# Three spacer tiles in SBUF that move the start addresses of a matmul kernel's tiles

## The chip, the cores and the metric

The kernel runs on one core of a Trainium2 chip. The metric is the device time of one execution in microseconds (us), lower is better.

## The reference

Two transformer-like parts run one after the other on 256 tokens of width 1024, in float32.

```python
h = h + hybrid_mixer(rmsnorm(h, norm1_w), w_in, ...)   # part 1: dilated attention and a state-space scan side by side
h = h + swiglu(rmsnorm(h, norm2_w), w_ffn_in, w_ffn_out)
...
# part 2: two layers over a stream x and a context c (256 tokens each), each layer:
# modulated rms_norm -> swiglu -> joint attention (kinds a, b, c, d) -> modulated rms_norm -> swiglu
def swiglu_2(h, w_gate, w_up, w_down):
    return (jax.nn.silu(h @ w_gate) * (h @ w_up)) @ w_down
```

Nearly all of the arithmetic is in the products `activations @ weights`: the input and output projections of the mixers and the three matrices of each swiglu, about 360 MB of weights, each read once.

## The kernel before

Activations lie feature by feature: a tile of 128 features holds a stream's 256 tokens as 256 columns of 4 bytes, 1024 bytes in each partition. Where the streams x and c go through the same weights, their columns lie side by side and a matmul has 512 columns (2048 bytes); a single stream makes 256.

A float32 product is made as three float32r matmuls. Weights and activations are each split into a high and a low part, `h` (ScalarE copies, L114 and L119) and `lo` (VectorE subtracts, L115 and L120), and `mm3_k` adds three products into one PSUM tile:

```python
nc.tensor.matmul(out, h[:, c], ah, start=first, stop=False)    # L133
nc.tensor.matmul(out, h[:, c], al, start=False, stop=False)    # L134
nc.tensor.matmul(out, lo[:, c], ah, start=False, stop=last)    # L135
```

The first tile is stationary (128 weight columns of 4 bytes, 512 bytes a partition), the second is moving. A unit of the program is one 512 KB slab of weights: a DMA from SyncE's queue into `wraw`, the split into `wh` and `wl`, and 8 steps of three matmuls. `run` writes the units in order and prepares two or three ahead. Five buffers each of `wraw`, `wh` and `wl` allow this. Between units it weaves attention, norms and, from the end of part 1 on, background work (the modulation vectors, L981).

Moving tiles are named after what they hold: `ah`/`al` are the normed activations, `hh`/`hl` a swiglu's hidden values, `aoh`/`aol` the attention's output in part 1, `ynh`/`ynl` three of the four groups of the scan's normed output in part 1 (the fourth reuses `aoh`/`aol`), `hq`/`lq` and `hk`/`lk` low-rank queries and keys in part 2. The products of the value projections (L1145 to L1147) are the other way round: activations are stationary and a weight slice of 256 or 320 columns moves. Attention itself uses plain float32 matmuls, with `q`, `k`, `pts`, `e`, `xdt` and the like.

SBUF is given out by pools. Each pool is a stretch of bytes in every partition, the next one begins where the last ended (rounded up to 32 bytes), and tiles follow each other within it. So the size of one small tile sets where all the tiles of later pools begin. Order of the pools: `cst`, `raw`, `wsplit`, `tmp`, `small`, then the streams, then those of a block that is under way (`block1` opens `b1a` with `ah`/`al` and `b1x`, which begins with `cw`).

Of the kernel before, what the change touches and what calls it, by code (L numbers as in the profile page):

```python
# [8 lines left out]
F32 = mybir.dt.float32  # L9
# [39 lines left out]
class Unit:  # L49


    def __init__(self, src, at, n, body, streams=None, lin=None, wide=False):
        self.src, self.at, self.n, self.body, self.streams, self.lin = src, at, n, body, streams, lin
        self.wide = wide
# [14 lines left out]
class Builder:  # L69
    def __init__(self, ctx, tc, A):  # L70
        self.tc, self.nc, self.A, self.ctx = tc, tc.nc, A, ctx
        nc = self.nc
        self.cst = self.pool(ctx, "cst", 1)
        self.raw_p = self.pool(ctx, "raw", 5)
        self.w_p = self.pool(ctx, "wsplit", 5)
        self.tp = self.pool(ctx, "tmp", 10)
        self.small = self.pool(ctx, "small", 2)
        self.comb, self.one_p = None, None
        self.ps = ctx.enter_context(tc.tile_pool(name="ps", bufs=4, space=PSUM))
        self.pa = ctx.enter_context(tc.tile_pool(name="pa", bufs=2, space=PSUM))  # L80
        self.pt = ctx.enter_context(tc.tile_pool(name="pt", bufs=2, space=PSUM))
        self.dram = ctx.enter_context(tc.tile_pool(name="scratch", bufs=1, space=DRAM))
        self.X, self.ACT, self.acc, self.bg, self.deferred = {}, {}, {}, [], []

        self.ones = self.cst.tile([128, 128], F32, name="ones")
        nc.vector.memset(self.ones, 1.0)
        self.cols = self.cst.tile([128, NCOL], F32, name="cols")
        self.ident = self.cst.tile([128, 128], F32, name="ident")

    def pool(self, ctx, name, bufs):  # L90
        return ctx.enter_context(self.tc.tile_pool(name=name, bufs=bufs))
# [357 lines left out]
def block1(K, start_mod):  # L449
    nc, tc, A = K.nc, K.tc, K.A  # L450
    ctx = ExitStack()
    K.one_p = K.pool(ctx, "b1a", 1)
    xpool = K.pool(ctx, "b1x", 1)
# [22 lines left out]

    tri = K.cst.tile([128, 128], F32, name="tri")
    nc.gpsimd.dma_start(tri, A["tri"])
    cw = xpool.tile([128, 120], F32, name="cw")
    at, _ = COLS["conv_w"]  # L480

    y_t = [xpool.tile([128, 4, T], F32, name=f"y{g}") for g in range(4)]
# [1191 lines left out]
def kernel(ctx, tc, A, parts=(1, 2)):  # L1674
# [20 lines left out]
    if 1 in parts:  # L1695
        block1(K, start_mod)
    else:
        start_mod()
# [198 lines left out]
```

## Time and profile before

| | before |
|---|---|
| median of 3 runs | 2523.09 us (2517.67 to 2523.85) |
| the profiled execution: its time | 2521.26 us |
| its span in the trace | 2519.5 us |
| TensorE (PE) matmul busy | 2459.8 us, 98% |
| weight loads (PEld) busy | 2122.6 us, 84% |
| VectorE (DVE) busy | 1642.6 us, 65% |
| ScalarE (ACT) busy | 1069.2 us, 42% |
| granted TensorE clock, mean | 0.986 |

A matmul's own duration covers its way through the array and overlaps with the next one's, and its end is modelled. What a matmul costs in a dense stream is therefore read as the distance from its start to the next one's start, and that is called its step below. Over a longer stretch it is the first and last start divided by the number of steps between.

### The profile page before, as it was taken

What the parts mean: (1) busy time and instruction counts of PE and PEld (TensorE: products, weight loads), DVE (VectorE), ACT (ScalarE), POOL (GpSimd) and SP (SyncE); (2) the same over time, 40 slices, a digit from 0 to 9 for tenths busy, and PEclk for the clock granted to TensorE, in tenths of its full rate; (3) what the DMA queues carried; (4) which work ended last, traced back from release to release, by engine and by line L of the source; (5) the groups of instructions that cost most, each with busy time, mean ns of one, the idle gap of its engine ahead of it and who ended that gap; (6) DMA issues with size and microseconds to landing.
All of it is one profiled execution on the core that took longest, in us unless ns stands there. A gap on an engine that the chain in (4) does not pass through costs nothing.

```text
span 2519.5 us, 38382 instructions
## 1 busy us (share of the span) xinstructions
PE 2459.8 (98%) x15104; PEld 2122.6 (84%) x15104; DVE 1642.6 (65%) x3009; ACT 1069.2 (42%) x1934; POOL 20.6 (1%) x30
## 2 busy tenths in 40 slices
PE   6999999999999999999999999999999999999999
PEld 6999999999988888886598888887888888866999
DVE  4667877787855665768667666657545455767554
ACT  4557565535522222436743222243222234555443
POOL 1000000000000000000000000000000000000000
PEclk9999999999999999999899999999999999999999
DMA  8545555676444554331024555434555422332553
GB/s 249 151 153 162 160 163 185 209 251 205 160 154 142 167 175 127 120 118 51 1 61 158 166 159 159 155 95 145 176 166 159 146 88 74 108 89 80 176 185 126
DMA packets 117252, 363.83 MB, mean 144 GB/s; under 512 B 21170, under 2 KB 28658, under 8 KB 117072
## 3 DMA queue, kind: packets, MB, share of 16 engines
q1 hardware_dynamic: 114512, 355.73, 44.4%
q0 software_dynamic: 1280, 3.45, 0.7%
q8 instruction: 119, 1.95, 0.3%
q10 hardware_dynamic: 1280, 2.20, 0.3%
q14 instruction: 61, 0.50, 0.1%
HBM read 359.33 MB, written 3.82 MB: 144 GB/s over the span
## 4 chain that ended last, share of the span: by engine, by line
PE 71%; DVE 2%; ACT 1%; issue 0%; DMA 0%; ACTq 0%
PE pm L133 21%; PE pm L134 21%; PE pm L135 20%; PE pt L1120 1%; PE pm L1319 1%; PE pa L1027 1%; PE pt L1051 1%; PE pa L1571 1%; PE pa L1335 1%; PE pm L1579 1%; PE pm L1259 0%; PE pa L1296 0%; PE pm L1601 0%; PE pm L1145 0%; PE pa L1147 0%; PE pa L1145 0%
## 5 line engine op out<-in xcount | busy, mean ns | idle before, releaser
L133 PE MATMUL pm<-ah,wh 128*128 128x256 f32 (+2 forms) x3096 | 1012.5, 329 | 21.6 <-ACT ah L355 11.2
L134 PE MATMUL pm<-al,wh 128*128 128x256 f32 (+2 forms) x3096 | 1007.8, 326 | 1.2 <-DVE al L356 1.2
L135 PE MATMUL pm<-ah,wl 128*128 128x256 f32 (+2 forms) x3096 | 1005.2, 325 | 0.0
L114 ACT CAST wh<-wraw 128x1024 fp32r<-128x1024 f32 (+4 forms) x535 | 540.5, 1013 | 1045.7 <-PE pm L134 853.9
L115 DVE TENSOR_TENSOR wl<-wraw,wh 128x1024 fp32r<-128x1024 f32 (+4 forms) x535 | 627.4, 1176 | 253.2 <-ACT wh L114 250.9
L133 PEld LDWEIGHTS pm<-ah,wh 128*128 128x128 f32 (+1 forms) x3096 | 587.9, 191 | 81.6 <-ACT ah L355 12.9
L134 PEld LDWEIGHTS pm<-al,wh 128*128 128x128 f32 (+1 forms) x3096 | 590.5, 191 | 54.4 <-DVE al L356 2.4
L135 PEld LDWEIGHTS pm<-ah,wl 128*128 128x128 f32 (+1 forms) x3096 | 590.4, 191 | 51.6 <-issue 1.4
L134 PE MATMUL pm<-hl,wh 128*128 128x512 f32 (+1 forms) x934 | 317.5, 340 | 0.0
L133 PE MATMUL pm<-hh,wh 128*128 128x512 f32 (+1 forms) x934 | 316.8, 339 | 0.0
L135 PE MATMUL pm<-hh,wl 128*128 128x512 f32 (+1 forms) x934 | 316.5, 339 | 0.0
L981 DVE SCALAR_TENSOR_TENSOR junk<-wraw,cactc 128x1024 f32<-128x1024 f32 x112 | 137.1, 1224 | 182.1 <-DMA wraw<-w_mod 181.9
L981 DVE SCALAR_TENSOR_TENSOR junk<-wraw,cactx 128x1024 f32<-128x1024 f32 x144 | 176.0, 1222 | 42.9 <-DMA wraw<-w_mod 40.3
L135 PEld LDWEIGHTS pm<-hh,wl 128*128 128x128 f32 x934 | 176.0, 188 | 21.1
L134 PEld LDWEIGHTS pm<-hl,wh 128*128 128x128 f32 x934 | 175.9, 188 | 21.2
L133 PEld LDWEIGHTS pm<-hh,wh 128*128 128x128 f32 x934 | 175.7, 188 | 21.2
L119 ACT CAST hh<-g 128x512 fp32r<-128x512 f32 (+1 forms) x113 | 59.2, 526 | 175.0 <-DVE g L413 174.9
L413 DVE TENSOR_TENSOR g<-g,pm 128x512 f32<-128x512 f32 (+1 forms) x113 | 64.0, 566 | 69.6 <-PE pm L135 68.1
L120 DVE TENSOR_TENSOR hl<-g,hh 128x512 fp32r<-128x512 f32 (+1 forms) x113 | 63.9, 567 | 0.3
L443 DVE SCALAR_TENSOR_TENSOR xc<-pm,mcol0c,xc 128x256 f32<-128x256 f32 x56 | 27.0, 481 | 56.0 <-PE pm L135 55.8
L409 ACT ACTIVATE g<-pm 128x512 f32<-128x512 f32 (+1 forms) x116 | 56.0, 488 | 2.5 <-PE pm L135 2.3
L1120 PEld LDWEIGHTS pt<-ident,e 128*128 128x128 f32 x272 | 30.7, 144 | 21.8 <-issue 18.7
(422 smaller groups left out, 2249.3 us busy)
## 6 DMA issues: line engine op xcount, KB each, us to landing
wraw<-w_mod SPq DMA_DIRECT2D x144, 512.0 KB, 3.9
wraw<-f1g SPq DMA_DIRECT2D x44, 512.0 KB, 4.0
wraw<-f1u SPq DMA_DIRECT2D x44, 512.0 KB, 4.1
wraw<-f2g SPq DMA_DIRECT2D x44, 512.0 KB, 3.6
wraw<-f2u SPq DMA_DIRECT2D x44, 512.0 KB, 3.8
wraw<-f1d SPq DMA_DIRECT2D x32, 512.0 KB, 3.9
wraw<-f2d SPq DMA_DIRECT2D x32, 512.0 KB, 3.6
wraw<-w_xbc SPq DMA_DIRECT2D x24, 512.0 KB, 3.6
```

Of the source, the lines that this page charges most:

```text
L114: nc.scalar.copy(h[:, :f], raw[:, :f])
L115: nc.vector.tensor_tensor(lo[:, :f], raw[:, :f], h[:, :f].bitcast(F32), op=ALU.subtract)
L119: self.nc.scalar.copy(h, src)
L120: self.nc.vector.tensor_tensor(lo, src, h.bitcast(F32), op=ALU.subtract)
L133: nc.tensor.matmul(out, h[:, c], ah, start=first, stop=False)
L134: nc.tensor.matmul(out, h[:, c], al, start=False, stop=False)
L135: nc.tensor.matmul(out, lo[:, c], ah, start=False, stop=last)
L409: nc.scalar.activation(half(g["g"], s), p, AF.Silu)
L413: nc.vector.tensor_tensor(t, t, p, op=ALU.mult)
L443: self.nc.vector.scalar_tensor_tensor(x, p, gate, x, op0=ALU.mult, op1=ALU.add)
L981: nc.vector.scalar_tensor_tensor(junk, raw, 1.0, K.cact[s], op0=ALU.mult, op1=ALU.mult, accum_out=K.mcol[layer, s][:, j:j + 1])
L1120: nc.tensor.transpose(p[:, j * 128:(j + 1) * 128], b, K.ident)
```

## The change

Three tiles that nothing reads are put in: 320 bytes in a pool of their own behind the weight buffers, and 160 and 352 bytes behind `cw` in `block1`, where `cw` itself grows from 480 to 512 bytes (160 + 352 = 512). VectorE fills each once, so that it counts as written.

```diff
         self.w_p = self.pool(ctx, "wsplit", 5)
+
+        self.gap(self.pool(ctx, "gap", 1), 320)
         self.tp = self.pool(ctx, "tmp", 10)
...
+    def gap(self, pool, n):
+
+        self.nc.vector.memset(pool.tile([128, n // 4], F32, name=f"gap{n}"), 0.0)
...
-    cw = xpool.tile([128, 120], F32, name="cw")
+    cw = xpool.tile([128, 128], F32, name="cw")[:, :120]
+    K.gap(xpool, 160)
+    K.gap(xpool, 352)
     at, _ = COLS["conv_w"]
```

Where the tiles begin in the built program, as the remainder of the address by 512 bytes (and by 1024 for those that the text needs); a tile's 256-column blocks follow at 1024 or 2048 bytes, so they begin at the same remainder:

| tiles | before | after |
|---|---|---|
| `wraw`, `wh`, `wl` (weights; stationary in L133 to L135, moving in L1145 to L1147) | 0xc0 | 0xc0 |
| `ah`, `al`, `hh`, `hl`: moving | 0x40 (by 1024: 0x40) | 0x180 (by 1024: 0x180) |
| `aoh`, `aol`: moving | 0x20 (by 1024: 0x220) | 0x180 |
| `ynh`, `ynl`: moving | 0x180 (by 1024: 0x380) | 0xe0 |
| `hq`, `lq`, `hk`, `lk`: moving | 0x60 | 0x1a0 |
| moving slices of `wh`, `wl`, 320 columns (by 1024) | 0xc0, 0x1c0, 0x2c0 | the same |
| part 1's `q`, `k`, `vt`, `pts`, `xdt`, `la` (float32) | 0x180 | 0xe0 |
| part 2's `e`, `pts` (float32) | 0xc0 or 0x120 | 0x0 or 0x60 |

The order of the instructions on the engines stays as it was, except on VectorE at the very start of the program. There the rows of the kernel before are (`ones` and `rel` are constants, `acc` and `sq` the first norm's sums):

```order
L86 MEMSET ones 128x128
L466 MEMSET rel 33x24
L879 MEMSET half 128x1
L946 MEMSET one 128x1
L889 TENSOR_SCALAR cw<-cols 128x120
L307 TENSOR_TENSOR acc<-acc,sq 128x256 x4
```

In the changed kernel the same place reads (line numbers behind the new lines are 2 to 8 higher):

```order
L94 MEMSET gap_67 128x80
L88 MEMSET ones 128x128
L472 MEMSET rel 33x24
L94 MEMSET gap_134 128x40
L94 MEMSET gap_136 128x88
L887 MEMSET half 128x1
L954 MEMSET one 128x1
L897 TENSOR_SCALAR cw<-cols 128x120
L313 TENSOR_TENSOR acc<-acc,sq 128x256 x4
```

Three fills are added ahead of the first work that waits for data; no other instruction is added, removed or moved.

## Rows read from the trace of the kernel before

**Rows 1.** The page: busy time by engine, and the chain that ended last.

```profile
span 2519.5 us, 38382 instructions
...
PE 2459.8 (98%) x15104; PEld 2122.6 (84%) x15104; DVE 1642.6 (65%) x3009; ACT 1069.2 (42%) x1934; POOL 20.6 (1%) x30
...
PE 71%; DVE 2%; ACT 1%; issue 0%; DMA 0%; ACTq 0%
PE pm L133 21%; PE pm L134 21%; PE pm L135 20%; PE pt L1120 1%; PE pm L1319 1%; PE pa L1027 1%; PE pt L1051 1%; PE pa L1571 1%; PE pa L1335 1%; PE pm L1579 1%; PE pm L1259 0%; PE pa L1296 0%; PE pm L1601 0%; PE pm L1145 0%; PE pa L1147 0%; PE pa L1145 0%
```

**Rows 2.** Waits: who waited, for whom; us in total, times, longest us.

```profile
ACT wh L114 <- PE pm L134: 853.9, 311, 7.1
...
PE pm L133 <- ACT ah L355: 11.2, 9, 1.6
```

**Rows 3.** Matmul groups of L133 by shape: count, busy us, mean ns, idle before.

```profile
L133 PE MATMUL pm<-ah,wh 128*128 128x256 f32 x1968 | 567.1, 292 | 21.6 <-ACT ah L355 11.2 <-ACT q L526 8.3 <-ACT ah L119 2.0
...
L133 PE MATMUL pm<-hh,wh 128*128 128x256 f32 x460 | 129.8, 282 | 0.0
...
L133 PE MATMUL pm<-aoh,wh 128*128 128x256 f32 x64 | 18.6, 291 | 0.3 <-ACT aoh L119 0.3
...
L133 PE MATMUL pm<-ynh,wh 128*128 128x256 f32 x96 | 26.7, 279 | 0.0
...
L133 PE MATMUL pm<-ah,wh 128*128 128x512 f32 x1112 | 440.5, 396 | 0.0
...
L133 PE MATMUL pm<-hh,wh 128*128 128x512 f32 x474 | 187.1, 395 | 0.0
```

**Rows 4.** Timeline of TensorE, 256 columns moving from 0x40: first and 25th start.

```profile
560.14 0.28 PE L133 MATMUL pm<-ah,wh 128*128 128x256 f32 x1
...
563.02 0.28 PE L133 MATMUL pm<-ah,wh 128*128 128x256 f32 x1
```

**Rows 5.** Windows: us; busy us (instructions) of PE, PEld, DVE, ACT, POOL; clock; DMA share, GB/s.

```profile
300.00:400.00 100.00, 99.00 (x878) 94.86 (x877) 82.06 (x160) 63.52 (x120) 0.00 (x0) 1.00 0.49 155
500.00:600.00 100.00, 100.00 (x836) 100.00 (x835) 83.58 (x128) 43.60 (x61) 0.00 (x0) 1.00 0.75 252
700.00:1000.00 300.00, 300.00 (x1292) 243.24 (x1291) 185.26 (x281) 75.63 (x93) 0.00 (x0) 1.00 0.48 152
...
2400.00:2500.00 100.00, 100.00 (x846) 100.00 (x844) 56.48 (x71) 43.31 (x62) 0.00 (x0) 1.00 0.54 173
```

**Rows 6.** Timeline, one unit: 0x180 (first, 26th), then 0x20 (first, 12th).

```profile
399.00 0.28 PE L134 MATMUL pm<-ynl,wh 128*128 128x256 f32 x1
...
401.83 0.28 PE L135 MATMUL pm<-ynh,wl 128*128 128x256 f32 x1
401.95 0.28 PE L133 MATMUL pm<-aoh,wh 128*128 128x256 f32 x1
...
403.25 0.28 PE L135 MATMUL pm<-aoh,wl 128*128 128x256 f32 x1
```

**Rows 7.** Timeline, 320 columns of weights moving: first and 23rd start.

```profile
1126.74 0.31 PE L1145 MATMUL pm<-wh,ah 128*128 128x320 f32 x1
...
1129.96 0.31 PE L1146 MATMUL pm<-wh,al 128*128 128x320 f32 x1
```

**Rows 8.** Timeline, 512 columns from 0x40: first and 25th start.

```profile
803.67 0.39 PE L133 MATMUL pm<-ah,wh 128*128 128x512 f32 x1
...
809.25 0.40 PE L133 MATMUL pm<-ah,wh 128*128 128x512 f32 x1
```

**Rows 9.** A window at the lower clock, columns as in rows 5.

```profile
2156.90:2158.60 1.70, 1.70 (x9) 1.70 (x9) 0.94 (x2) 0.00 (x0) 0.00 (x0) 0.50 0.54 165
```

**Rows 10.** Timeline of that window, 256 columns from 0x60: first and 8th start.

```profile
2156.91 0.41 PE L134 MATMUL pm<-lq,wh 128*96 128x256 f32 x1
...
2158.40 0.41 PE L135 MATMUL pm<-hq,wl 128*96 128x256 f32 x1
```

**Rows 11.** A fill on VectorE: duration ns min/median/max, first and last start us.

```profile
L86 DVE MEMSET ones<- x1: 165/165/165, 0.8 to 0.8; 128x128 f32 x1
```

## The prediction

> **What bounds the kernel now.** I read the page first. TensorE is busy for 98% of the span, the three lines of the split product hold 62% of the chain that ended last, and no other engine has more than 2% of it [rows 1]. The waits say the same from the other side: the longest wait for TensorE is ScalarE's, 853.9 us in which the next weights' split could start and the weight buffer is still in use by a matmul, while TensorE's longest own wait sums to 11.2 us [rows 2]. So the time is, to a few per cent, the number of matmuls times the step from one start to the next, and I looked for what sets that step.
>
> The groups give the counts [rows 3]. Each of L133, L134 and L135 has as many. With 256 columns and a start that the change moves to 0x180 there are (1968 + 460 + 64) x 3 = 7476 matmuls, with 512 columns (1112 + 474) x 3 = 4758.
>
> The steps come from the timeline. 256 columns from 0x40: 2.88 us over 24 steps, 120.0 ns [rows 4]; later, 846 matmuls are seen in 100 us, two of them cut by the window's ends, so about 118.5 ns [rows 5]. I use 119.2. [...]
>
> The telling rows are in one unit at 399 us. Weights, engines and the second operand's place are the same, only the moving tile changes: `ynh` and `ynl`, which begin at 0x180, step by 2.83 us / 25 = 113.2 ns, and `aoh` and `aol` right behind them, at 0x20, by 1.30 / 11 = 118.2 ns [rows 6]. Weight slices of 320 columns, from 0xc0 and its neighbours, take 3.22 us / 22 = 146.4 ns where the columns are 133.3: 13.1 ns too many [rows 7]. So 0x20, 0x40 and 0xc0 cost 11.5 to 13 ns over the columns, 0x180 costs 6.6. That the start is the cause is an inference from four starts. 512 columns were only seen from 0x40 in bulk: 5.58 us / 24 = 232.5 ns, 19.2 over the 213.3 of the columns [rows 8].
>
> [...]
>
> **The change, part by part.**
>
> *256 columns from 0x180.* The row is there: 113.3 ns for 119.2. That is 5.9 x 7476 = 44.1 us.
>
> *512 columns from 0x180.* No row shows it. The least gain that fits the mechanism: the gain of 5.9 comes once a matmul, so 226.6 ns, which is also twice 113.3; that is 28.1 us. The most: the columns alone, 213.3 ns, 19.2 x 4758 = 91.4 us. Which of the two is nearer? From 0x40 the excess grows from 12.5 ns at 256 columns to 19.2 at 512, so part of it goes with the columns, about 6.7 per 256, and the rest, near 6, comes once. From 0x180 256 columns have 6.6 in all, which leaves room for one of these two parts and not for both. Between the matmuls a new stationary tile has to be taken in whatever the start, so I take it that the once-a-matmul part stays and the part that goes with the columns vanishes: 213.3 + 6.7 = 220.0 ns, 12.5 x 4758 = 59.5 us.
>
> *`ynh` and `ynl` leave 0x180* for 0xe0, where nothing was measured. If 0xe0 is like the other starts they lose what the rest gain: 96 x 3 x 5.9 = 1.7 us. At the other end they lose nothing.
>
> *Plain float32 matmuls* (attention, head sums) get other starts too, some leaving 0x180. They are lines of 1% of the chain or less, about 125 us together [rows 1]; a twentieth of that either way is 6 us. I take 0, since no row separates their starts.
>
> *Weights and the value projections* stay at 0xc0: 0.
>
> *Three fills on VectorE.* The largest fill now takes 165 ns [rows 11], so three smaller ones are under 0.5 us. They run while the first loads are on their way, hence 0; uncovered they cost 0.5.
>
> *What is given back.* A faster TensorE asks sooner for weights. In the dense stretches of 512 columns VectorE has 185.3 of 300 us and DMA a share of 0.48, so nothing is near its limit. Around 300 to 600 us VectorE is at 82 to 84%, and at 500 to 600 us DMA at 0.75 with 252 GB/s [rows 5]. From 100 to 640 us there are about 8.4 matmuls a us, 4500, which gain 27 us. If VectorE set the pace there all 27 would be lost, if the buffers bridge its bursts none. It would go from 84 to 88%, so I take a quarter, 7 us.
>
> Sum: 44.1 + 59.5 - 1.7 - 7 = 94.9 us. Against the profiled execution, 2521.3 us, this gives 2426.4; the median of the runs shown is 1.8 above it, so 2428 us.
>
> [...]
>
> **The rivals.**
>
> 1. *The forecast*: both widths gain, 512 by more than 256. About 2428 us.
> 2. *512 gains just 5.9 ns*, since the loss is at the start of a matmul and the growth with columns stays. For it: twice 113.3 is 226.6. Against it: the excess at 0x180 would then have no fixed part at all. 59.5 becomes 28.1: 2459 us.
> 3. *512 gains nothing*: its loss is another one than that of 256, as its different excess allows. 2428 + 59.5 = 2487 us.
> 4. *Nothing happens*: the step of `ynh` comes from something else, its place high in the partition or its four-block tiles. For it: there is one quick tile pair only. Against it: `hq`, as high and at 0x60, is not quick, though the stretch quoted for it is at the lower clock. 2523 us. [...]
> 5. *Slower*: the pattern repeats over 1024 bytes, not 512. The quick tiles stood at 0x380 by 1024, the new ones will stand at 0x180, half a turn away, and could be as far above today's step as 0x380 is below it: 5.9 x (7476 + 4758) = 72 us more, 2595. It decides as soon as the step from 0x180 lies over 119.2 and 232.5 ns. Against it: the 320-column slices begin at three places by 1024, and their 22 steps in a row average the same excess as the rest [rows 7], so no place of 1024 stood out among the slow ones.
>
> **How the numbers follow.** Rival 1 has 58%, 2 has 21%, 3 has 7%, 4 has 8%, 5 has 6%. The predicted time is the first's. Its own range comes from the 512 step at 216 (19 us less) to 224 ns (19 more) and from 0 to 20 us given back: 2402 to 2460. The range of 8 in 10 is carried up to take in rival 2 with half of those 27 us given back, 2459 + 7 = 2466, and a little for the float32 lines: 2402 to 2470; it leaves out rivals 3, 4 and 5, 21%. A measurement here tells about 0.3%, 7.6 us, from no change. Rivals 1, 2 and 3 are faster by more than that: 0.86. Rival 4 is no change: 0.08. Rival 5 is slower: 0.06.
>
> **What would show it.** In the profile after, steps of 113 ns in the 256-column stretches at 500 to 600 us (some 880 matmuls per 100 us, for 836) and in the last 100 us; 220 ns in the 512-column ones (some 1360 in 300 us for 1292, where 226.6 would give 1325); `ynh` slower than now, near 119, and `aoh` quicker. If ScalarE's wait for TensorE shrinks and TensorE's waits for `wh` or `wl` grow between 100 and 640 us, the given-back term is right in kind. The forecast is wrong if the 512 step stays over 228, or if VectorE's or DMA's lateness at 300 to 600 us eats the first term.

## The result, and the profile after

The changed kernel takes 2509.48 us (median of 11 runs, 2498.57 to 2517.63) where the kernel before takes 2522.72 us (11 runs, 2516.40 to 2529.99). The ratio is 0.9946, with a 95% interval of 0.9931 to 0.9962: 13 us faster. Forecast were 2428 us, 95 us faster, with a range that ends at 2470. The direction was right, the size was not. The profiled execution of the changed kernel took 2511.2 us and has a span of 2509.1, 10.4 us less than before [rows 1]. The same lines stand 6 higher now: L139, L140 and L141 are the matmuls that were L133 to L135.

The page of the changed kernel reads as it did before. TensorE is still the bound.

```profile
span 2509.1 us, 38385 instructions
...
PE 2440.5 (97%) x15104; PEld 2097.5 (84%) x15104; DVE 1641.9 (65%) x3012; ACT 1067.5 (43%) x1934; POOL 20.6 (1%) x30
...
PE 69%; DVE 4%; ACT 2%; issue 1%; DMA 0%; ACTq 0%; DVEq 0%; SPq 0%
PE pm L139 20%; PE pm L140 20%; PE pm L141 20%; PE pt L1128 1%; PE pa L1035 1%; DVE wl L121 1%; PE pm L1327 1%; PE pt L1059 1%; PE pa L1579 1%; PE pm L1587 1%; DVE al L362 1%; PE pa L1343 1%; DVE y L357 1%; PE pm L1267 1%; PE pa L1304 0%
```

The windows of the changed kernel (columns as in rows 5) show by stage what became of the two large terms.

```profile
500.00:600.00 100.00, 96.79 (x830) 95.66 (x829) 84.23 (x129) 43.53 (x62) 0.00 (x0) 1.00 0.75 253
700.00:1000.00 300.00, 300.00 (x1287) 241.71 (x1286) 182.83 (x276) 75.93 (x93) 0.00 (x0) 1.00 0.48 152
2400.00:2500.00 100.00, 100.00 (x851) 100.00 (x851) 56.69 (x74) 42.11 (x59) 0.00 (x0) 1.00 0.52 159
```

With 512 columns (700 to 1000 us) there are 1287 matmuls in 300 us where there were 1292 [rows 5]: the step grew. At the end, 851 for 846: the 256-column step shrank by 0.7 ns only. From 500 to 600 us there are 830 for 836, fewer than before, and TensorE is no longer busy all the time.

The timeline of TensorE in the changed kernel gives the steps: two stretches of 256 columns and one of 512, each by its first start and the start 18 steps on.

```profile
610.35 0.28 PE L139 MATMUL pm<-ah,wh 128*128 128x256 f32 x1
...
612.39 0.28 PE L139 MATMUL pm<-ah,wh 128*128 128x256 f32 x1
...
801.44 0.39 PE L139 MATMUL pm<-ah,wh 128*128 128x512 f32 x1
...
805.64 0.39 PE L139 MATMUL pm<-ah,wh 128*128 128x512 f32 x1
...
2400.42 0.28 PE L140 MATMUL pm<-al,wh 128*128 128x256 f32 x1
...
2402.54 0.28 PE L140 MATMUL pm<-al,wh 128*128 128x256 f32 x1
```

The same tile at the same start steps by 2.04 / 18 = 113.3 ns near 610 us and by 2.12 / 18 = 117.8 ns near 2400 us. 256 columns have two states, and only one is the row of `ynh` on which the forecast rested [rows 6]. 512 columns step by 4.20 / 18 = 233.3 ns, which is no gain at all over [rows 8].

Over the whole trace I took each step that is at most a quarter longer than its columns, at the 26.7 ns for 64 columns that *The step by columns* measures, and called what is longer a stall; its excess is what it has over its columns. The moved 256-column matmuls went from a mean of 119.0 to 115.7 ns, which over 7476 of them is -25 us. The 512-column ones went from 232.7 to 233.3: +3 us. `ynh` and `ynl` went from 113.9 to 116.8: +0.8. The stalls' excess went from 80.8 to 90.5: +9.7. These make -11.5, beside -10.4 of the span.

The largest loss in one place is not a wait. These are the windows from 250 to 270 us of the kernel before and then of the changed kernel (columns as in rows 5):

```profile
250.00:270.00 20.00, 20.00 (x131) 16.60 (x130) 17.22 (x39) 8.32 (x16) 0.00 (x0) 1.00 0.21 67
250.00:270.00 20.00, 20.00 (x91) 16.11 (x90) 11.34 (x27) 4.73 (x10) 0.00 (x0) 0.66 0.10 39
```

In the changed kernel's profiled run the granted clock is 0.50 from 253.4 to 267.0 us, and the kernel before has 1.00 there. At 0.50 a step of 256 columns takes 213 ns in both traces and so counts as a stall in the sum above. Counted by the starts of the same matmuls in both traces, 6.1 us are lost between 250 and 270 us. Just before the clock fell, split matmuls alternated with products of 8 partitions (`pt<-ub,gts`), as they do in the kernel before. Why it fell in the one and not in the other stays open. In another place it is the other way round (from 1230 to 1260 us 0.66 before and 0.78 after), and over the whole span the mean is 0.986 in both.

### The profile page after: what moved, and what is told of

It reads as the page before. It is cut to its first block, busy times and chain, and to the rows that moved or that the text cites. A ratio compares the mean times of both kernels' runs of the same rounds, so it can differ in the third digit from the quotient of the medians.

```text
span 2509.1 us, 38385 instructions
## 1 busy us (share of the span) xinstructions
PE 2440.5 (97%) x15104; PEld 2097.5 (84%) x15104; DVE 1641.9 (65%) x3012; ACT 1067.5 (43%) x1934; POOL 20.6 (1%) x30
## 4 chain that ended last, share of the span: by engine, by line
PE 69%; DVE 4%; ACT 2%; issue 1%; DMA 0%; ACTq 0%; DVEq 0%; SPq 0%
PE pm L139 20%; PE pm L140 20%; PE pm L141 20%; PE pt L1128 1%; PE pa L1035 1%; DVE wl L121 1%; PE pm L1327 1%; PE pt L1059 1%; PE pa L1579 1%; PE pm L1587 1%; DVE al L362 1%; PE pa L1343 1%; DVE y L357 1%; PE pm L1267 1%; PE pa L1304 0%
## 5 line engine op out<-in xcount | busy, mean ns | idle before, releaser
L139 PE MATMUL pm<-ah,wh 128*128 128x256 f32 (+2 forms) x3096 | 1007.7, 328 | 25.3 <-ACT ah L361 11.0
L140 PE MATMUL pm<-al,wh 128*128 128x256 f32 (+2 forms) x3096 | 1001.8, 324 | 1.5 <-DVE al L362 1.5
L141 PE MATMUL pm<-ah,wl 128*128 128x256 f32 (+2 forms) x3096 | 999.9, 324 | 0.0
L120 ACT CAST wh<-wraw 128x1024 fp32r<-128x1024 f32 (+4 forms) x535 | 540.4, 1013 | 1028.8 <-PE pm L140 833.4
L139 PEld LDWEIGHTS pm<-ah,wh 128*128 128x128 f32 (+1 forms) x3096 | 587.2, 191 | 87.4 <-ACT ah L361 12.5
L140 PEld LDWEIGHTS pm<-al,wh 128*128 128x128 f32 (+1 forms) x3096 | 591.2, 191 | 56.1 <-DVE al L362 2.8
L141 PEld LDWEIGHTS pm<-ah,wl 128*128 128x128 f32 (+1 forms) x3096 | 588.8, 190 | 52.9 <-issue 1.7
L140 PE MATMUL pm<-hl,wh 128*128 128x512 f32 (+1 forms) x934 | 316.5, 339 | 0.4 <-DVE hl L126 0.4
L139 PE MATMUL pm<-hh,wh 128*128 128x512 f32 (+1 forms) x934 | 316.0, 338 | 0.7 <-DVE xx L449 0.7
L141 PE MATMUL pm<-hh,wl 128*128 128x512 f32 (+1 forms) x934 | 315.9, 338 | 0.0
L140 PEld LDWEIGHTS pm<-hl,wh 128*128 128x128 f32 x934 | 176.4, 189 | 22.2 <-DVE hl L126 0.6
L139 PEld LDWEIGHTS pm<-hh,wh 128*128 128x128 f32 x934 | 175.7, 188 | 22.4 <-issue 0.8
L141 PEld LDWEIGHTS pm<-hh,wl 128*128 128x128 f32 x934 | 175.6, 188 | 21.5
```

The lines of the kernel that those rows point to most:

```text
L120: nc.scalar.copy(h[:, :f], raw[:, :f])
```

## The experiments

My theory after the result was that the start of a moving operand does not count by itself. What counts is how far it lies from the start of the stationary operand. The rivals were the forecast's own reading, the moving start alone; the weight load as the whole of the excess; and, for the period, 512 bytes against 256.

**The matmuls alone, from every start.** A program of dense matmuls in the kernel's pattern (two with `wh`, one with `wl`); the model is left out.

```diff
+    ah = p.tile([128, 5120], F32R, name="ah")
...
+    def steps(at, name, n, stride, mo, wo, m, reps):
...
+                w = slice(wo * 8 + k * 128, wo * 8 + k * 128 + m)
+                c = slice(mo * 8 + k * stride, mo * 8 + k * stride + n)
...
+                nc.tensor.matmul(o[:m, :n], wh[:, w], ah[:, c], start=i == 0, stop=False)
+                nc.tensor.matmul(o[:m, :n], wh[:, w], al[:, c], start=False, stop=False)
+                nc.tensor.matmul(o[:m, :n], wl[:, w], ah[:, c], start=False, stop=i == total - 1)
```

> This program leaves the model out and holds matmuls alone: runs of 120 (first visit) or 72 (second visit) of the same triples as L133 to L135, each run with one start of the moving tile (16 starts, 32 bytes apart, named a to p; c is 0x40, m is 0x180) and the weights at 0xc0, at 512 columns, at 256 columns 1024 bytes apart and at 256 columns 2048 bytes apart. Then eight starts of the weights, and runs with 32 weight columns in place of 128. Nothing else uses SBUF. If the moving start alone sets the step: 256 columns step by 113 ns at m and 118 to 120 at c and most others, at both visits; 512 columns step by 232 to 233 at both c and m, and some other start may show 220 to 227. If the distance between moving and stationary start sets it: moving m with weights at 0xc0 (distance 0xc0) equals moving c with weights at 0x180 (distance 0xc0 too). If it is a state into which the stream falls after a stall, the two visits of one start differ by 4 to 5 ns. If the weight load is what disturbs the moving stream, 512 columns with 32 weight columns step by 214 to 220 ns whatever the start.

The view of a tile gives, for each run of matmuls, their count, the least, median and largest duration of one in ns, and the first and the last start in us. A line takes every third matmul, so 40 of them span 117 steps, 32 span 93 and 24 span 69. The letter behind `m` is the moving start in units of 32 bytes (`a` is 0x0, `g` 0xc0, `m` 0x180), the one behind `w` the stationary start. `wide` has 512 columns, `dense` 256; `x` is a first visit, `y` a second.

```profile
L1749 PE MATMUL widex_mg_wg<-ah,wh x40: 389/389/395, 186.3 to 212.8; 128*128 128x512 f32 x40
L1749 PE MATMUL widex_mi_wg<-ah,wh x40: 388/388/398, 241.5 to 268.3; 128*128 128x512 f32 x40
L1749 PE MATMUL widex_mm_wg<-ah,wh x40: 393/394/394, 353.1 to 380.4; 128*128 128x512 f32 x40
...
L1749 PE MATMUL densex_mg_wg<-ah,wh x40: 280/283/283, 549.0 to 563.0; 128*128 128x256 f32 x40
L1749 PE MATMUL densex_mi_wg<-ah,wh x40: 280/280/283, 577.5 to 591.3; 128*128 128x256 f32 x40
L1749 PE MATMUL densex_mm_wg<-ah,wh x40: 276/276/286, 634.4 to 647.7; 128*128 128x256 f32 x40
...
L1749 PE MATMUL densey_mm_wg<-ah,wh x24: 281/281/288, 1210.0 to 1218.1; 128*128 128x256 f32 x24
...
L1749 PE MATMUL widez_mc_we<-ah,wh x32: 393/396/398, 1501.2 to 1522.9; 128*128 128x512 f32 x32
L1749 PE MATMUL widez_mm_we<-ah,wh x32: 389/389/398, 1678.7 to 1699.8; 128*128 128x512 f32 x32
```

With the weights at 0xc0 as in the kernel, 512 columns take 26.5 us / 117 = 226.5 ns from 0xc0 and 27.3 / 117 = 233.3 from 0x180, the start that the change chose. The start 0x180 with the weights moved to 0x80 takes 21.1 / 93 = 226.9 (`widez_mm_we`), and 0x40 with those weights 21.7 / 93 = 233.3. So the same start is best or worst by where the weights lie. The two moving starts with all eight weight starts go by the distance in this way, at both widths. The 16 moving starts with the weights at 0xc0 repeat after 256 bytes (512 columns take 27.3 / 117 = 233.3 ns from 0x80 and from 0x180), but for small differences between visits: 512 columns from 0x140 took 233.4 ns at the first visit and 232.4 at the second. By the distance d, moving start less stationary start modulo 256, the steps are, from the starts to the ns:

| | d = 0 | 0x40 | 0x80 | 0xc0 | odd multiples of 0x20 |
|---|---|---|---|---|---|
| 512 columns, ns | 226.7 | 228.9 | 232.4 | 233.3 | 233.3 to 234.3 |
| 256 columns, ns | 120.0 | 117.8 | 118.7 | 113.3 or 117.8 | 116.7 to 120 |

The kernel before has d = 0x80 for `ah` and `hh`, the changed one d = 0xc0. That is the best distance at 256 columns and nearly the worst at 512. At d = 0xc0 the first visit of 256 columns ran at 113.3 and the second at 117.8 from the starts to the ns (8.1 us over 69 steps by the row above, which is rounded to 0.1 us). With only 32 weight columns to load, 512 columns still take 231.6 ns, so the weight load is not their whole excess over the columns. The width of the weight tile has a part in what the distance does, though: with 32 weight columns the moving starts 0x0, 0x40, 0x80 and 0x180, which are the distances 0x40, 0x80 and twice 0xc0, all step by 113.3 ns at 256 columns and by 230.7 to 231.7 at 512. With 256 columns, blocks 1024 or 2048 bytes apart make no difference (at d = 0 the rows give 14.0 / 117 = 119.7 ns here for 1024 and, for 2048, 8.3 / 69 = 120.3 in the run by columns below), which leaves nothing of rival 5's 1024 bytes.

**In the kernel: start against distance.** Two kernels, each shown against the changed one. In the first the gap of 320 bytes stands ahead of the weight buffers, so that the moving tiles keep the change's 0x180 and the weights go to 0x0: the distance of the kernel before. In the second the moving tiles stay at 0x40 as before and only the weights go to 0x0: d = 0x40.

```diff
+        self.gap(self.pool(ctx, "gap", 1), 320)
         self.raw_p = self.pool(ctx, "raw", 5)
         self.w_p = self.pool(ctx, "wsplit", 5)
-
-        self.gap(self.pool(ctx, "gap", 1), 320)
```

> The 320 bytes stand ahead of the raw weight buffers, so that weights and moving tiles shift alike: moving tiles begin at 0x180 as in the changed kernel, wh and wl at 0x0 instead of 0xc0. The distance from weights to moving tiles is then that of the kernel before. Moving start alone: as the changed kernel, 2509 us, 256-column steps of 113 to 118 ns, 512-column steps of 231 and 236. Distance: as the kernel before, 2523 us, 120 ns and 228 to 241. Weights' own start with a part in it: neither.

```diff
+        self.gap(self.pool(ctx, "gap", 1), 320)
         self.raw_p = self.pool(ctx, "raw", 5)
         self.w_p = self.pool(ctx, "wsplit", 5)
-        self.gap(self.pool(ctx, "gap", 1), 320)
+        self.gap(self.pool(ctx, "gap2", 1), 192)
...
-    cw = xpool.tile([128, 128], F32, name="cw")[:, :120]
-    K.gap(xpool, 160)
-    K.gap(xpool, 352)
+    cw = xpool.tile([128, 120], F32, name="cw")
```

> The kernel before with 320 bytes ahead of the raw weight buffers and 192 behind the split ones: the moving tiles begin as before (0x40 by 512, all 512 bytes later), wh and wl at 0x0 instead of 0xc0. Moving start alone: as the kernel before, 2523 us, 256-column steps of 118 to 122 ns, 512-column steps of 232.7. Distance or the weights' own start: steps differ from those by 2 ns or more, and the time by 10 us or more either way.

The first took 2524.35 us (12 runs) beside 2521.04 of the kernel before, a ratio of 1.0013 (0.9998 to 1.0029): with the change's moving starts and the old distance nothing is gained. The second took 2499.45 us (6 runs), 0.9906 (0.9885 to 0.9926): with the old moving starts and a new distance there is more gain than the change brought. Its windows show 1312 matmuls in 300 us of 512 columns. The moving start alone is refuted, the distance holds. The value projections of 256 columns, where the weights move and the activations are stationary, go the same way: stalls left out, they step by 118.9 ns in the kernel before and 118.9 in the first of these two (d = 0x80 in both), by 117.7 in the changed kernel (0x40) and by 114.8 in the second (0xc0).

```profile
700.00:1000.00 300.00, 300.00 (x1312) 246.19 (x1311) 186.94 (x285) 77.53 (x98) 0.00 (x0) 1.00 0.49 154
```

**The period.** The changed kernel with a gap of 64 bytes in place of 320, so that these moving tiles begin 256 bytes earlier, at 0x80.

```diff
-        self.gap(self.pool(ctx, "gap", 1), 320)
+        self.gap(self.pool(ctx, "gap", 1), 64)
```

> The changed kernel with 64 bytes in place of 320 behind the weight buffers: the moving tiles begin at 0x80 instead of 0x180, 256 bytes earlier; the weights stay at 0xc0, the gaps in block1 too. If the steps repeat over 256 bytes of distance, the steps are those of the changed kernel (113 to 118 ns at 256 columns, 233.3 at 512) and the time is 2509 us. If they repeat over 512, as the change's own words have it, the distance is another one and the steps differ: 512 columns off 233.3 by 1 ns or more, the time off 2509 by 5 us or more.

It took 2507.11 us (6 runs) beside 2526.42, 0.9926 (0.9907 to 0.9944), with 512 columns at 233.3 ns and 256 at a mean of about 114.5. That is the changed kernel again: by 256 bytes, not 512.

**The step by columns.** The matmuls alone once more, with 128 to 512 columns at four distances; then 16 stretches of 256 columns at d = 0xc0, two behind each of eight kinds of short ones (512 or 256 columns at each distance), and 24 such stretches, all but the first entered behind a wait for VectorE. The model is left out.

```diff
+    for n in (128, 192, 256, 320, 384, 448, 512):
+        for d in (0, 2, 4, 6):
+            steps(at, f"cols{L[n // 64]}_d{L[d]}", n, 512, 6 + d, 6, 128, 3)
...
+    o = ps.tile([128, 512], F32, name="sole", tag="sole", bufs=1)
+    for j in range(24):
+        for r in range(16):
```

> Matmuls alone again, the model left out. [...] Then 256 columns at distance 0xc0 right behind short runs of other widths and distances, and behind 24 waits of growing length for VectorE: if the two states are entered by what went before, visits show either 113.3 or 117.8 throughout, and both occur; if one is an accident of a single run, all show one.

The view of a tile again; 24 matmuls of a line span 69 steps, 16 span 45. `d` to `i` are 192 to 512 columns, `da` is distance 0 and `dg` 0xc0.

```profile
L1749 PE MATMUL colsd_de<-ah,wh x24: 272/274/277, 96.4 to 104.1; 128*128 128x192 f32 x24
L1749 PE MATMUL colse_dg<-ah,wh x24: 276/276/286, 138.2 to 146.0; 128*128 128x256 f32 x24
L1749 PE MATMUL colsf_dg<-ah,wh x24: 307/308/310, 178.0 to 188.1; 128*128 128x320 f32 x24
L1749 PE MATMUL colsg_da<-ah,wh x24: 333/334/346, 188.6 to 200.6; 128*128 128x384 f32 x24
...
L1749 PE MATMUL colsi_da<-ah,wh x24: 389/389/397, 297.2 to 312.9; 128*128 128x512 f32 x24
L1749 PE MATMUL colsi_dg<-ah,wh x24: 392/393/398, 346.8 to 362.9; 128*128 128x512 f32 x24
...
L1749 PE MATMUL aftericx<-ah,wh x16: 279/281/281, 391.3 to 396.6; 128*128 128x256 f32 x16
L1749 PE MATMUL afteriex<-ah,wh x16: 276/276/276, 413.7 to 418.8; 128*128 128x256 f32 x16
```

From the starts to the ns, the least step at any distance is 113.3 ns for 256 columns, 146.7 for 320, 173.3 for 384, 200.0 for 448 and 226.7 for 512. From 320 to 448 columns each 64 more take 26.7 ns. At that rate the columns alone are 106.7 ns at 256, 133.3 at 320 and 213.3 at 512. These are the times over which the prediction counts its excess (12.5 ns is 119.2 less 106.7). They are an estimate from the 26.7 ns, and the 213 ns of 256 columns at a clock of 0.50 [rows 9, 10], twice 106.7, agree with it. The least steps are then the columns and 6.7 ns for each begun 256. Below 256 columns this does not hold: 192 step by 111.7 ns. A cost of 6.7 ns once a matmul would give 220.0 at 512, where 226.7 were measured; steps in proportion to the columns would, from 226.7 at 512, give 141.7 at 320, where 146.7 were measured. (128 columns stood in the program's first stretch and stepped by 213 ns; I make nothing of them.)

The last two rows are the same matmuls at the same distance behind short stretches of 512 columns at 0x40 and at 0x80: 5.3 / 45 = 117.8 ns and 5.1 / 45 = 113.3. What went before does not settle it alone: behind 256 columns at 0x80 the first visit kept 117.8 and the second 113.3. Of the 24 stretches, 23 of them behind a wait, 19 settled at 113.3 and 5 at 117.8 within their first five steps, and each then kept its step. So the state is set where a dense stretch is entered.

**Distances by width.** What the table would have: d = 0 where 512 columns move, d = 0xc0 where 256 do. The joint tile of both streams gets a second view 192 bytes further on for stretches of one stream, and gaps of 192 bytes, not shown here, move the other tiles of one stream. In the built program 1716 of the 7476 matmuls of 256 columns still begin at d = 0, since they take one stream's half of a tile that lies for 512.

```diff
-        self.gap(self.pool(ctx, "gap", 1), 320)
+        self.gap(self.pool(ctx, "gap", 1), 128)
...
+        flat = [p.tile([128, KB * 2 * T + 64], F32R, name="a" + n) for n in "hl"]
+        view = lambda t, at: t[:, at:at + KB * 2 * T].rearrange("p (b s t) -> p b s t", b=KB, s=2)
+        self.comb, self.alone = [[view(t, at) for t in flat] for at in (0, 48)]
...
+            return tuple(t[:, :, BOTH.index(s)] for t in (self.alone if alone else self.comb))
```

> From the matmul-only run: what counts is the distance from the stationary start to the moving start by 256 bytes. 512 columns step by 226.7 ns at distance 0, 228.9 at 0x40, 232.4 at 0x80 (the kernel before), 233.3 at 0xc0 (the changed kernel); 256 columns by 120.0, 117.8, 118.7, and 113.3 or 117.8 (two states). Here the weights stay at 0xc0, the tiles of 512 columns begin at distance 0, the tiles of 256 columns at distance 0xc0 (the streams' shared tile gets 256 bytes more, so that a lone stream can begin 0xc0 further on). Distance theory: 512-column steps of 226.7, 256-column steps of 113 to 118, time 2509 - 6.6 x 4758 ns = 2478 us. If a start by 512 mattered, or if the two widths disturbed each other, 512 columns would stay over 230 and the time at 2505 to 2512.

Beside it ran the single gap of 128 bytes that puts all of these tiles at d = 0:

```diff
-        self.gap(self.pool(ctx, "gap", 1), 320)
+        self.gap(self.pool(ctx, "gap", 1), 128)
...
-    K.gap(xpool, 160)
-    K.gap(xpool, 352)
```

> One gap of 128 bytes behind the weight buffers in place of the three: all moving tiles begin at 0xc0, distance 0 for both widths. Distance theory: 512 columns step by 226.7, 256 columns by 120.0, so against the kernel before 6.0 x 4758 ns = 28.5 us less and 0.9 x 7476 ns = 7 us more, 2500 us. If only the moving start counted, 0xc0 would be a new start with no forecast; the matmul-only run at that start gives the same steps, so this run tells whether its steps hold inside the kernel.

By width: 2478.03 us (5 runs) beside 2523.85, 0.9805 (0.9782 to 0.9828). All at zero: 2501.32 us (6 runs), 0.9916 (0.9897 to 0.9934). Both medians landed within 2 us of what the table gave. For the first this is in part luck: its runs lie from 2467.05 to 2478.76 us, and in its profiled run the long stretches among the 1716 matmuls left at d = 0 step by 120.0 ns, slower than in the changed kernel, while the last long stretch of 256 columns ran in the quicker state (885 matmuls in 100 us, for 851). It beats both the kernel before and the changed one. Its window of the dense 512-column stretch has 1325 matmuls for the 1287 of the changed kernel, 300 / 1325 = 226.4 ns:

```profile
700.00:1000.00 300.00, 300.00 (x1325) 248.47 (x1325) 189.22 (x289) 78.80 (x99) 0.00 (x0) 1.00 0.51 155
```

With all at zero the 512-column window is the same and 256 columns pay for it, 832 in 100 us, 120 ns a step:

```profile
500.00:600.00 100.00, 99.88 (x832) 99.62 (x831) 85.31 (x133) 44.45 (x64) 0.00 (x0) 1.00 0.77 256
700.00:1000.00 300.00, 300.00 (x1326) 248.39 (x1325) 192.85 (x292) 77.47 (x95) 0.00 (x0) 1.00 0.51 160
```

**What gives time back around 500 us.** TensorE's own waits from 480 to 640 us in the changed kernel (the same view of the kernel before names none):

```profile
PE pm L139 <- DVE g L419: 1.7, 3, 1.2
PE pm L139 <- DVE xx L449: 1.1, 2, 0.7
PE pm L140 <- DVE hl L126: 0.4, 1, 0.4
PE pt L344 <- DVE rs L322: 0.3, 1, 0.3
PE pt L336 <- DVE acc L313: 0.3, 1, 0.3
```

The timeline of VectorE, and then of TensorE, at the longest of them:

```profile
559.15 1.22 DVE L989 SCALAR_TENSOR_TENSOR junk<-wraw,cactc 128x1024 f32<-128x1024 f32 x1 [2.41 <-DMA wraw<-w_mod]
...
560.42 1.22 DVE L989 SCALAR_TENSOR_TENSOR junk<-wraw,cactx 128x1024 f32<-128x1024 f32 x1
...
561.57 1.22 DVE L121 TENSOR_TENSOR wl<-wraw,wh 128x1024 fp32r<-128x1024 f32 x1
562.71 0.41 DVE L419 TENSOR_TENSOR g<-g,pm 128x256 f32<-128x256 f32 x1
...
563.17 0.38 PE L139 MATMUL pm<-ah,wh 128*128 128x256 f32 x1 [1.16 <-DVE g L419]
```

VectorE stands 2.41 us until a modulation weight has landed; two multiplications with it and one weight split are ahead of `g` in its queue, and TensorE waits 1.16 us for `g`. Either end of that queue could be the cause: the work, or the late load. Two kernels part them. The first leaves out the first layer's multiplications for the stream x (its result there is a fill of zeros) and keeps every load; the second reads an eighth of each of that layer's modulation weights and multiplies only that.

```diff
+        if layer == 0 and s == "x":
+            nc.vector.memset(K.mcol[layer, s], 0.0)
...
+        if layer == 0:
+            who = who[:1]
```

> The changed kernel with half of the first layer's modulation vectors left out (the x stream's, 72 multiplications of 1.22 us on VectorE; a zero fill stands in for them), loads and order otherwise the same. If VectorE's lateness is what gives back the gain at 480 to 640 us, TensorE's waits for VectorE there (g, xx and hl, 3.2 us by the waits, some 6 us by the steps) go to under 1 us. If the loads are late, they stay. If a stall is what moves the 256-column stream between its two states, this stretch keeps one state, 117.6 or 113.3, for longer than in the changed kernel.

```diff
-            raw = K.load_raw(K.A[f"w_mod{layer}"][j])
+            f = 128 if layer == 0 else D
+            raw = K.load_raw(K.A[f"w_mod{layer}"][j][:, :f])
```

> The changed kernel with seven eighths of the first layer's modulation weights left out (each of 72 loads is 64 KB instead of 512 KB, and VectorE multiplies 128 columns of them instead of 1024). Taking away half of VectorE's background work left TensorE's stalls at 480 to 640 us in place, and VectorE waited 31.0 us for the modulation weights there, 14.1 us in the changed kernel. If the late loads make VectorE's queue late, and the matmuls behind it, TensorE's waits for VectorE there (g, xx, hl, wl: 3.2 us) go under 1 us and the long steps from 6 us to under 2. If they come from the order of the units alone, they stay.

With less work, one run of 2508.12 us, the waits stay: 3.7 us for `xx` and `wl`, where it would be under 1 us if VectorE's work were the cause. TensorE's waits in the same stretch, and the window:

```profile
PE pm L139 <- DVE xx L449: 2.1, 2, 1.5
PE pm L141 <- DVE wl L121: 1.6, 1, 1.6
...
480.00:640.00 160.00, 155.83 (x1341) 154.94 (x1340) 111.81 (x171) 77.71 (x116) 0.00 (x0) 1.00 0.68 226
```

With less to load, one run of 2506.91 us, they are gone:

```profile
PE pt L344 <- DVE rs L322: 0.3, 1, 0.3
PE pt L336 <- DVE acc L313: 0.3, 1, 0.3
...
480.00:640.00 160.00, 159.45 (x1405) 159.12 (x1405) 108.41 (x210) 84.79 (x124) 0.00 (x0) 1.00 0.62 186
```

VectorE is busy for about as long in both, 111.8 and 108.4 us of 160, where it has 129.9 in the changed kernel. So its busy share is not enough to explain the stalls. The two kernels differ in more than that, though: in the traffic, 226 and 186 GB/s, and in the time of one multiplication with a modulation weight, 1.22 and 0.29 us. And VectorE's own wait for these weights from 480 to 640 us did not go away with the small loads. These are the changed kernel, the one with less work and the one with less to load:

```profile
DVE junk L989 <- DMA wraw<-w_mod: 14.1, 13, 2.4
...
DVE junk L993 <- DMA wraw<-w_mod: 31.0, 14, 4.4
...
DVE junk L990 <- DMA wraw<-w_mod: 26.1, 13, 3.4
```

So either the traffic or the long multiplications right behind a late weight can be what holds TensorE up; these runs do not part the two. The whole times, one run each, lie within the changed kernel's own 2498.57 to 2517.63 us, so they show no gain.

## Why the prediction was wrong in size

- **512 columns, forecast -59.5 us, measured +3.** This is the step that failed: "I take it that the once-a-matmul part stays and the part that goes with the columns vanishes". No run shows such a split. Of its sum, 213.3 + 6.7, the 213.3 is what 512 columns come to at the measured 26.7 ns for 64; no run shows 6.7 as all that is left over it, nor a step of 220.0. The least step at 512 is 226.7 ns, twice the 113.3 of 256 columns and 13.3 over the columns, and it comes at distance 0; the change went to 0xc0, where it is 233.3. Rival 2's step, 226.6, is the least one, but at another distance than the change's and for another reason. Rival 3, that 512 gains nothing, is what happened to this width. It stood at 7% with 2487 us, and the smaller 256-column gain makes up most of the way from there to 2509.
- **The start as the cause.** The text called it "an inference from four starts". All of those had the weights at 0xc0, so start and distance could not be told apart. The first kernel of the pair tells them apart: the change's moving starts with the old distance give 1.0013.
- **256 columns, forecast -44.1 us, measured -25.** The 5.9 ns rested on 113.2 of `ynh` [rows 6]. That 256 columns step quicker from 0x180 came out, but only because the weights stayed at 0xc0, so the reason was not the one given; and the size is off: at d = 0xc0 there are two states, 113.3 and 117.8 ns, and the mean over the changed kernel is 115.7, 3.4 ns less than before. That the row of `ynh` was in the quicker state was luck. The last 100 us of the profiled run were in the slower one, with 851 matmuls; the kernel of "The period", at the same distances, has 885 there. That last stretch has 1555 matmuls, so by an estimate its state alone is worth 1555 x 4.5 ns = 7 us.
- **`ynh` and `ynl`, forecast +1.7, measured +0.8.** Right in sign; 116.8 ns at 0xe0 and not 119.
- **Fills and plain float32, forecast 0.** Nothing in the two traces speaks against it: the terms measured sum to -11.5 and the span fell by 10.4.
- **Value projections, forecast 0 because the weights stay.** Their stationary `ah` and `al` moved, so their distance changed too. The term was small all the same: 1.2 ns a step at 256 columns.
- **Given back, forecast +7, measured +9.7.** Right in size, and in the stretch that was named, but not in kind. ScalarE's wait for TensorE fell from 853.9 [rows 2] to 833.4 us, as foreseen. But the largest loss there, 6.1 us between 250 and 270 us, goes with the granted clock, for which the forecast had no term. TensorE's new waits from 480 to 640 us, 3.2 us, are for `g`, `xx` and `hl` and not for `wh` or `wl`, and VectorE's busy share, on which that term was built, is not enough to explain them: with 111.8 us for 129.9 they stay.
- **Rival 4**, that the place of `ynh` high in the partition or its four-block tiles made it quick, is excluded: `ah` steps by 113.3 ns at the same distance, in the changed kernel and in the bare matmuls.
- **Rival 5, the period of 1024 bytes**, is excluded: the steps repeat after 256.

What stays open: why the distance acts as it does inside the chip, what picks the state of 256 columns, and why the clock fell near 253 us. Separate distances for `wh` and `wl` were not tried.

## What to carry to other kernels

Where TensorE is the bound and steps a few per cent above its columns, measure the step as a table over the distance between moving and stationary operand, for each width by itself, before moving any tile: here the same distance was the best at 256 columns and among the worst at 512. A quick stretch in a trace shows what is possible, not what makes it quick, as long as another address stayed the same in all rows read. A small program of the bare matmuls gave steps that then held inside two rearranged kernels: at 512 columns 226.7 ns in the program, 226.2 and 226.4 in the kernels' windows.

## What the hardware showed that was not expected

- At the starts tried, all multiples of 32 bytes, the step of dense float32r matmuls (128 by 128 weights) goes with the distance of the two operands' starts by 256 bytes, and not with either start: 226.7 to 234.3 ns at 512 columns, 113.3 to 120.0 at 256. At 192 columns (111.7 ns) and at 320 (146.7) the four distances tried step alike. With 32 weight columns three distances step alike at 256 columns too, by 113.3.
- From 256 to 512 columns the least step is 26.7 ns for every 64 columns and 6.7 ns more for each begun 256: 113.3 ns at 256, 146.7 at 320, 226.7 at 512.
- At distance 0xc0, 256 columns hold either of two steps, 113.3 or 117.8 ns, for as long as the stretch is dense; 5 of 23 entries behind a wait led to the slower. The longest stretch of the changed kernel, from 2322 to 2505 us, kept 117.8 throughout.
